# Dividing after the product instead of before it: one core's attention heads, with the reciprocals turned through DRAM

## The chip, the cores and the metric

The kernel runs on one core of one Trainium2 chip. The metric is the device time of one execution in microseconds (us). The engines are named as in the profile: PE is TensorE, DVE is VectorE, ACT is ScalarE, POOL is GpSimd, SP is the SyncE queue from which nearly all DMAs are issued.

## The reference

One decoder layer on 512 tokens of width 2048. After an RMSNorm, one projection feeds three mixers: A (8 heads of 64, three dilated windows mixed by their softmax denominators), B (a convolution of 31 taps over 512 channels, LayerNorm, swish), C (16 query heads on 2 key/value heads, window 128, one learned sink per head). The mixers' 2048 outputs go through `w_out` and are added to x; a second RMSNorm and a SwiGLU feed-forward block follow. What the change touches is the softmax of A and C, cut here to its core:

```python
p = jnp.exp(s - m[..., None])
denom = jnp.sum(p, axis=-1)
if sinks is not None:
    denom = denom + jnp.exp(sk - m)
o = jnp.einsum('nbhgqk,nbkhd->nbqhgd', p, vb)
o = o / denom_t[..., None]
```

## The kernel before, in words

All activations lie transposed: channels on the 128 partitions, the 512 tokens along the free axis. A float32 matrix product is made of three fast matmuls: each operand is split into a high and a low part (`wh`/`wl` for weights, `hh`/`hl` for the normed input, `mh_`/`ml_` for the mixers' rows), and `mm3` (L322 to L324) adds high by high, high by low and low by high.

**Stages.** The input projection makes 30 column tiles of 128 (`PROJ`); each is 16 contraction steps of three matmuls, fed by two weight units of 128 x 1024. While PE works through them, the other engines bring the mixers along in its shadow, and PE takes the small attention matmuls in between. From about 400 us on, PE does the `w_out` product: for each of 16 output tiles first the eight row tiles of `ROWS[:8]` (c0 to c6, half 0), later the other eight (a0, a1, b2, b1, b0, b3, a2, a3, half 1). The feed-forward block fills the rest, from about 580 us on.

**Order.** The order on every engine is written by a clock of the program, `Ticks`: `ticks.after(n, fn)` puts a step n ticks ahead, and the loop over matmuls calls `tick()` after every 6 of them in the projections and in half 0 of `w_out`, after every 12 in half 1. What a tick issues is appended to each engine's queue in that order, and each engine works its queue in order. A step whose input is late holds up all that stands behind it on its engine.

**A head** (`attention`, `head`) runs by one tuple of tick distances, `C_TICKS` or `A_TICKS`; their last entry `we` is the distance from the softmax weights' last split to their product with v. The steps of a head: scores on PE (`c6s`, `a0s`); maximum on DVE; exponentials on ACT into a slot `c6e` or `a0e`; the division on DVE (`packed_norm` for C, `norm` for A); transposes on PE (`c6t`, `a0t`, called flips here); split of the transposed weights into high and low (`c6hp`/`c6lp`, `a0ph`/`a0pl`), which for C are then spread by POOL's masked copies into `c6ph`/`c6pl` (L870, L873); the product with v on PE (`weigh`, L940 and L941, `c6o`, eight matmuls); copy of its two halves into `mix` by ACT (`out_high`) and DVE (L954). One row tile holds two heads, h = 0 and 1. `split_mix` (L994, L995) splits a finished row tile into `mh_`/`ml_`. For rows that come late (a2, a3), it is a tick after the row is complete.

**Slots.** Nearly every tile of 128 x 512 comes from one pool of 73 slots (`N_SLOTS`). A new tile gets a slot whose old tile has been read for the last time, and its first writer waits for that last reader. So the pool adds waits between steps that have nothing to do with each other, and which ones depends on the whole order of allocations.

**DMA.** SP issues in order. A DMA uses one of eight completion semaphores in turn and is issued when the one before it on that semaphore has landed. Small per-token factors are turned across partitions through DRAM in the kernel before already: `leave` (L642) writes a 128 x 16 tile, `back` (L647) reads it, and for keys `back` (L714) reads rows back broadcast over 64 partitions.

Of the kernel before, what the change touches and what calls it, by code (L numbers as in the profile page):

```python
# [9 lines left out]
F32 = mybir.dt.float32  # L10
# [4 lines left out]
ALU = mybir.AluOpType  # L15

P = 128
T = 512
NT = T // P
D = 2048  # L20
KT = D // P
HD = 64
HALF = (slice(0, HD), slice(HD, 2 * HD))
# [16 lines left out]
SD, KD, VD, EV = 9, 6, 12, 1  # L40


C_TICKS = (1, 6, 2, 2, 2, 3, 5, 1, 4)
A_TICKS = (0, 8, 2, 1, 3, 1, 3, 1, 5)


# [70 lines left out]
def kernel(ctx: ExitStack, tc: tile.TileContext, xT, wi, wo, wgu, wd, cst_in, outT):  # L117
    nc = tc.nc
    cp = ctx.enter_context(tc.tile_pool(name="consts", bufs=1))
# [16 lines left out]
    ticks = Ticks()  # L136

    def slot(name, dt=F32, cols=T):
        return sp.tile([P, cols], dt, name=name, tag="s")
# [11 lines left out]
    sums = defaultdict(list)  # L151
# [23 lines left out]
    def up_block(pair, m, half, j):  # L175
# [4 lines left out]
    bufs = {"A": dict(zip(("21", "11", "s", "22"), ("21a", "22a", "sa", "22b"))),  # L180
            "B": dict(zip(("21", "11", "s", "22"), ("21b", "11", "12", "sb")))}

    for n in range(2 * NBLOCKS):
# [15 lines left out]
        bufs = {c: {"21": b["22"], "11": b["21"], "s": b["s"], "22": b["11"]} for c, b in bufs.items()}  # L199
# [6 lines left out]
    for t, (g, r) in enumerate(DOWN):  # L206
# [7 lines left out]
        for k in ("21A", "11A", "21B", "11B", "22A", "22B", "12A", "12B"):  # L214
            c = k[2]
# [14 lines left out]
        bufs = {c: {"21": b["22"], "11": b["21"], "s": b["s"], "22": b["11"]} for c, b in bufs.items()}  # L230
# [255 lines left out]
    for k in range(KT):  # L486
# [9 lines left out]
        elif k < 4 or k % 2 == 0:  # L496
            wh, wl = next_unit()
            o = 0
# [294 lines left out]
    def attention(kind, box, mix, mi, heads):  # L793
        ready, every, step, s1, sx, s2, fl, ev, we = C_TICKS if kind == "c" else A_TICKS

        if mi in ROWS[-2:]:
            fl, we = fl + 2, we + 3
        name = mi
        us = UNITS[kind]
        st = {}  # L800

        def head(h):
            es = {}
            d = cp.tile([P, 4, NT], F32, name=f"{name}d{h}", tag="soft", bufs=6)
            mx, nm, den, rd = (d[:, i] for i in range(4))
            banks = {}

# [32 lines left out]
            def packed_norm():  # L840
                nc.vector.tensor_add(den, den, mx)
                nc.vector.reciprocal(rd, den)
                by = es["e"].rearrange("p (i c) -> p i c", c=P)
                nc.vector.tensor_mul(by, by, rd[:, :, None].to_broadcast([P, NT, P]))

            def packed_flip():
                b = bank(f"{name}t{h}")
# [43 lines left out]

            def norm(u):
                e = es[u]
                s = slice(us[u][0][0], us[u][-1][0] + 1)
                for i, k0, n, o in us[u]:
                    nc.vector.scalar_tensor_tensor(e[:, o:o + n], e[:, o:o + n], 1.0, mult_a[:, T - n:],
                                                   op0=ALU.mult, op1=ALU.mult, accum_out=den[:, i:i + 1])
                nc.vector.reciprocal(rd[:, s], den[:, s])
                for i, k0, n, o in us[u]:
                    nc.vector.tensor_scalar(e[:, o:o + n], e[:, o:o + n], rd[:, i:i + 1], None, op0=ALU.mult)  # L900

            ph, pl = {}, {}

# [42 lines left out]
            def out_high(b):  # L946
                if h == 0:
                    st["mix"] = slot(f"mix_{mi}")
                nc.scalar.copy(st["mix"][HALF[h]], b[HALF[1 - h]])
                ticks.after(EV, out_rows, b)  # L950

            def out_rows(b):
                m = st["mix"]
                nc.vector.tensor_add(m[HALF[h]], m[HALF[h]], b[HALF[h]])  # L954
                if h == 1:
                    mix[mi] = m
                    if late:
                        ticks.after(1, split_mix, mi)

            at_v = (len(us) - 1) * step + s1 + sx + s2 + fl + len(TBANKS[kind]) - 1 + ev + EV + we  # L960
            t0 = max(ticks.now + ready, head_at[0], box["q at"] - s1, box["k at"], box["v at"] - at_v)
            head_at[0] = t0 + every
            t0 -= ticks.now
            for u in range(len(us)):
                tu = t0 + u * step
                ticks.after(tu, scores, u)
                if kind == "c":
                    ticks.after(tu + s1, pack, u)
                    continue
                ticks.after(tu + s1, top, u)  # L970
                ticks.after(tu + s1 + sx, exps, u)
                ticks.after(tu + s1 + sx + s2, norm, u)
            tu = t0 + (len(us) - 1) * step + s1 + sx
            if kind == "c":
                ticks.after(tu, packed_exps)
                ticks.after(tu + s2, packed_norm)
                ticks.after(tu + s2 + fl, packed_flip)
            else:
                for t in range(len(TBANKS[kind])):
                    ticks.after(tu + s2 + fl + t, flip, t)  # L980
            ticks.after(t0 + at_v, weigh)

        head(0)
        head(1)


    mix, late = {}, []
# [34 lines left out]
    for name in PROJ[HEAD4:]:  # L1022
        kind, what, j = name[0], name[1], name[2:]
        if name == PROJ[-2]:
            for n, row in enumerate(ROWS[:8]):
                ticks.after(6 + n, split_mix, row)
        b = project(name)
        if kind == "b":
            ticks.after(0, glu_u if what == "u" else glu, int(j), b)
            continue  # L1030
        if kind == "c":
            box = Heads(shared) if j else shared
        else:
            box = boxes.setdefault(j, {})
        if what == "k":
            do_k(box, b, name, 1 if kind == "c" else 0)
        elif what == "v":
            do_v(box, b, name)
        else:
            do_q(box, b, name)  # L1040
        if what == "q":
            if kind == "a":
                boxes.pop(j)
            attention(kind, box, mix, kind + j, (int(j), int(j) + 8) if kind == "c" else None)
# [85 lines left out]
    for half in range(2):  # L1130
        for i, n in enumerate(OUT_ORDER[half]):
# [4 lines left out]
            for kk in range(8):  # L1136
# [4 lines left out]
                s = slice(kk * P, (kk + 1) * P)  # L1141
# [552 lines left out]
```

## Time and profile before

| | |
|---|---|
| median of 3 runs | 1843.22 us (1843.0 to 1843.69) |
| profiled execution, its own time | 1845.39 us |
| span of its trace | 1843.6 us |
| granted TensorE clock | 1.00 |
| busy: PE, DVE, ACT, POOL | 1835.2, 1445.8, 1312.1, 1026.2 us |
| DMA | 398924 packets, 334.61 MB |

The span is the time from the first to the last instruction in the trace; 1.8 us of the profiled execution lie outside it. Busy time is the sum of the durations in the records, and matmuls overlap in the array, so their records (389 ns for 128x512) are longer than the distance at which they start. Rows of the timeline give start, duration, engine, line, operation and tiles; a bracket at the end gives the idle time before the instruction and what ended it.

### The profile page before, as it was taken

The numbers are of one execution on the slowest core, as the hardware profiler recorded it, in microseconds if no ns is written. First come the engines' busy times: TensorE is split into PE (matmuls) and PEld (weight loads), VectorE is DVE, ScalarE is ACT, GpSimd is POOL, SyncE is SP. The second block draws the span as 40 slices with busy tenths as digits, with TensorE's granted clock in tenths as the row PEclk, the third lists the DMA queues.
The fourth block names the chain that finished last, engine by engine and source line by source line (L and its number), as shares of the span: only waits on it lengthen the run. The fifth ranks groups of instructions, "written<-read, shape, count | busy, mean of one in ns | idle before, by whom it ended". The sixth has DMA issues, their size and how long they took to land.

```text
span 1843.6 us, 26502 instructions
## 1 busy us (share of the span) xinstructions
PE 1835.2 (100%) x8314; PEld 1522.4 (83%) x8314; DVE 1445.8 (78%) x2063; ACT 1312.1 (71%) x1784; POOL 1026.2 (56%) x790
## 2 busy tenths in 40 slices
PE   9999999999999999999999999999999999999998
PEld 7888888888888888888888888888888888888887
DVE  6789988997689877778777787777777777777777
ACT  6345554553458788888888888888887778777775
POOL 0126644110003557886788767878676558776552
PEclk9999999999999999999999999999999999999999
DMA  7353345353343457677867778677687679877735
GB/s 276 87 150 93 87 121 153 107 161 116 124 149 103 115 151 191 188 213 182 225 187 200 201 188 226 181 209 199 182 273 258 204 225 295 257 254 260 240 119 110
DMA packets 398924, 334.61 MB, mean 181 GB/s; under 512 B 184256, under 2 KB 326720, under 8 KB 398784
## 3 DMA queue, kind: packets, MB, share of 16 engines
q1 hardware_dynamic: 398208, 332.14, 62.3%
q8 instruction: 66, 1.08, 0.3%
q10 hardware_dynamic: 576, 0.79, 0.1%
q14 instruction: 74, 0.61, 0.1%
HBM read 258.46 MB, written 65.98 MB: 176 GB/s over the span
## 4 chain that ended last, share of the span: by engine, by line
PE 95%; DVE 3%; DMA 1%; issue 0%; ACT 0%; SPq 0%; POOL 0%; DVEq 0%; POOLq 0%; ACTq 0%
PE out L1281 15%; PE out L1279 15%; PE out L1282 15%; PE out L1544 7%; PE out L1546 7%; PE out L1545 7%; PE o L322 3%; PE o L323 3%; PE o L324 3%; PE cq L322 2%; PE cq L324 2%; PE cq L323 2%; PE in L324 1%; PE in L323 1%; PE in L322 1%; PE aq L322 1%
## 5 line engine op out<-in xcount | busy, mean ns | idle before, releaser
L1279 PE MATMUL out<-wh,h 128*128 128x512 f32 x1232 | 479.2, 389 | 0.0
L1281 PE MATMUL out<-wl,h 128*128 128x512 f32 x1232 | 479.2, 389 | 0.0
L1282 PE MATMUL out<-wh,h 128*128 128x512 f32 x1232 | 479.2, 389 | 0.0
L1279 PEld LDWEIGHTS out<-wh,h 128*128 128x128 f32 x1232 | 231.2, 188 | 48.1
L1282 PEld LDWEIGHTS out<-wh,h 128*128 128x128 f32 x1232 | 231.2, 188 | 48.0
L1281 PEld LDWEIGHTS out<-wl,h 128*128 128x128 f32 x1232 | 231.2, 188 | 47.9
L1545 PE MATMUL out<-wl,a 128*128 128x512 f32 x620 | 240.4, 388 | 0.1
L1544 PE MATMUL out<-wh,a 128*128 128x512 f32 x620 | 240.4, 388 | 0.0
L1546 PE MATMUL out<-wh,a 128*128 128x512 f32 x620 | 240.3, 388 | 0.0
L289 ACT CAST wh<-w 128x1024 fp32r<-128x1024 f32 (+2 forms) x94 | 96.9, 1031 | 121.6 <-PE o L323 48.0
L1554 DVE TENSOR_TENSOR y<-y,out 128x512 f32<-128x512 f32 x192 | 128.5, 684 | 47.8 <-PE out L1546 46.1
L263 DVE TENSOR_TENSOR wl<-w,wh 128x1024 fp32r<-128x1024 f32 (+2 forms) x95 | 115.0, 1211 | 30.9 <-ACT wh L289 27.9
L1545 PEld LDWEIGHTS out<-wl,a 128*128 128x128 f32 x620 | 116.4, 188 | 24.5 <-DVE wl L285 0.5
L1546 PEld LDWEIGHTS out<-wh,a 128*128 128x128 f32 x620 | 116.4, 188 | 23.8
L1544 PEld LDWEIGHTS out<-wh,a 128*128 128x128 f32 x620 | 116.4, 188 | 23.8
L573 DVE SCALAR_TENSOR_TENSOR y<-bu,cst,y 128x511 f32<-128x511 f32 (+14 forms) x120 | 92.0, 767 | 1.3
L322 PE MATMUL o<-mh_c,wh 128*128 128x512 f32 x128 | 51.1, 399 | 0.2 <-DVE xr L1073 0.2
L322 PE MATMUL cq<-hh,wh 128*128 128x512 f32 x128 | 50.3, 393 | 0.0
L324 PE MATMUL o<-mh_c,wl 128*128 128x512 f32 x128 | 50.0, 391 | 0.0
L323 PE MATMUL o<-ml_c,wh 128*128 128x512 f32 x128 | 50.0, 390 | 0.0
L323 PE MATMUL cq<-hl,wh 128*128 128x512 f32 x128 | 49.9, 390 | 0.0
L324 PE MATMUL cq<-hh,wl 128*128 128x512 f32 x128 | 49.9, 390 | 0.0
(2351 smaller groups left out, 4766.5 us busy)
## 6 DMA issues: line engine op xcount, KB each, us to landing
od<-a SPq DMA_DIRECT2D x154, 256.0 KB
a<-od SPq DMA_DIRECT2D x154, 256.0 KB
w<-in_wi SPq DMA_DIRECT2D x58, 512.0 KB
w<-in_wo SPq DMA_DIRECT2D x32, 512.0 KB
x<-in_xT SPq DMA_DIRECT2D x16, 256.0 KB
xr<-in_xT SPq DMA_DIRECT2D x16, 256.0 KB
x2d<-xr SPq DMA_DIRECT2D x16, 256.0 KB
z<-x2d SPq DMA_DIRECT2D x64, 64.0 KB
```

What stands on the lines that cost most here:

```text
L263: fn(*args)
L289: (nc.vector.tensor_copy if u == 0 else nc.scalar.copy)(hi[:, :n], t[:, :n])
L322: nc.tensor.matmul(out, wh, xh, start=start, stop=False)
L323: nc.tensor.matmul(out, wh, xl, start=False, stop=False)
L324: nc.tensor.matmul(out, wl, xh, start=False, stop=stop)
L1279: nc.tensor.matmul(b, x[:, high], wh[:, s], start=c == f == 0 and q in (7, 1, 5, 2), stop=False, skip_group_check=True)
L1281: nc.tensor.matmul(b, x[:, high], wl[:, s], start=False, stop=False, skip_group_check=True)
L1282: nc.tensor.matmul(b, x[:, low], wh[:, s], start=False, stop=c == f == 1, skip_group_check=True)
L1544: nc.tensor.matmul(b[:, lo:hi], x[:, high], wh[:, s], start=start, stop=False, skip_group_check=True)
L1545: nc.tensor.matmul(b[:, lo:hi], x[:, high], wl[:, s], start=False, stop=False, skip_group_check=True)
L1546: nc.tensor.matmul(b[:, lo:hi], x[:, low], wh[:, s], start=False, stop=last, skip_group_check=True)
L1554: getattr(eng, op)(t, t, src)
```

## The change

The exponentials are no longer divided. `packed_norm` keeps the sum and one reciprocal per head; `norm` of A keeps the masked sums and takes one reciprocal of 128x4 for the head in place of three small ones. A tick later `sums_leave` writes the 128x4 reciprocals into a row of 512 in DRAM (element by element: neighbours in DRAM come from different partitions). When both heads of a row tile are in DRAM, `sums_back`, two ticks ahead of the second head's product with v, reads the two rows back, each broadcast over the 64 partitions of its head, into a slot `by`. A tick after the row tile is complete, `scale_out` multiplies it once by `by`, and only then is it handed on. For late rows `split_mix` follows one tick after that. `we` of C goes from 4 to 6: the products of C with v, and with them their copies, come two ticks later, and the finished row tile a third.

```diff
-C_TICKS = (1, 6, 2, 2, 2, 3, 5, 1, 4)
+C_TICKS = (1, 6, 2, 2, 2, 3, 5, 1, 6)
...
-        st = {}
+        st = {"sums": tc.dram_tile([2, T], F32, name=f"{name}sums")}
+
+        def sums_leave(h, rd):
+            nc.sync.dma_start(st["sums"][h].rearrange("(i p) -> p i", p=P), rd)
+
+        def sums_back():
+            st["by"] = slot(f"{name}by")
+            for h in range(2):
+                nc.sync.dma_start(st["by"][HALF[h]], st["sums"][h:h + 1].to_broadcast([HD, T]))
+
+        def scale_out():
+            m = st["mix"]
+            nc.vector.tensor_mul(m, m, st.pop("by"))
+            mix[mi] = m
+            if late:
+                ticks.after(1, split_mix, mi)
...
-            d = cp.tile([P, 4, NT], F32, name=f"{name}d{h}", tag="soft", bufs=6)
+            d = cp.tile([P, 4, NT], F32, name=f"{name}d{h}", tag="soft", bufs=8)
...
                 nc.vector.reciprocal(rd, den)
-                by = es["e"].rearrange("p (i c) -> p i c", c=P)
-                nc.vector.tensor_mul(by, by, rd[:, :, None].to_broadcast([P, NT, P]))
+                ticks.after(1, sums_leave, h, rd)
...
-                nc.vector.reciprocal(rd[:, s], den[:, s])
-                for i, k0, n, o in us[u]:
-                    nc.vector.tensor_scalar(e[:, o:o + n], e[:, o:o + n], rd[:, i:i + 1], None, op0=ALU.mult)
+                if u == len(us) - 1:
+                    nc.vector.reciprocal(rd, den)
+                    ticks.after(1, sums_leave, h, rd)
...
                 if h == 1:
-                    mix[mi] = m
-                    if late:
-                        ticks.after(1, split_mix, mi)
+                    ticks.after(1, scale_out)
...
             ticks.after(t0 + at_v, weigh)
+            if h == 1:
+                ticks.after(t0 + at_v - 2, sums_back)
```

In the changed file the lines of `attention` stand 13 to 15 further down: L940 and L941 become L953 and L954, DVE's addition L954 becomes L967, the scores L814 and L815 become L829 and L830, POOL's L870 and L873 become L884 and L887, the exponential L889 becomes L903, the flips L916 become L929, and `scale_out` is L812.

PE at the product of row tile c6's second head with v (`c6o`, at about 328 us before), with the scores (`a0s`) and the flips (`a0t`) of row tile a0's first two heads around it; `ak` is a projection. Before:

```order
L940 MATMUL c6o_3507<-c6ph_3414,cv_746 128x256
L941 MATMUL c6o_3507<-c6pl_3440,cv_746 128x256
L940 MATMUL c6o_3507<-c6ph_3417,cv_746 128x256
L941 MATMUL c6o_3507<-c6pl_3443,cv_746 128x256
L940 MATMUL c6o_3507<-c6ph_3417,cv_746 128x128
L941 MATMUL c6o_3507<-c6pl_3443,cv_746 128x128
L814 MATMUL a0s_3516<-ak0h_2956,aq_3097 128x384
L815 MATMUL a0s_3516<-ak0l_2957,aq_3097 128x384
L322 MATMUL ak_3392<-hh_410,wh_3304 128x512
```

The same place in the changed kernel, from the third matmul of the product on:

```order
L953 MATMUL c6o_3563<-c6ph_3438,cv_746 128x256
L954 MATMUL c6o_3563<-c6pl_3472,cv_746 128x256
L953 MATMUL c6o_3563<-c6ph_3441,cv_746 128x256
L954 MATMUL c6o_3563<-c6pl_3475,cv_746 128x256
L953 MATMUL c6o_3563<-c6ph_3441,cv_746 128x128
L954 MATMUL c6o_3563<-c6pl_3475,cv_746 128x128
L929 MATMUL a0t_3572<-ident,a0e_3392 128x128 x2
L929 MATMUL a0t_3572<-ident,a0e_3462 128x128
L929 MATMUL a0t_3572<-ident,a0e_3500 128x128
```

The product has moved past the scores and 12 projection matmuls, so that the flips of a0, which read three slots of exponentials, follow straight behind it.

POOL at the last masked copies into that product's low operand, with the semaphores that each waits for, before:

```order
L870 AFFINE_SELECT c6pl_3443<-c6lp_3412 128x2x128 [waits DMAHW4_49,DMAHW3_49,DMAHW7_49,DMAHW0_49,DVE_49]
L873 AFFINE_SELECT c6pl_3443<-c6lp_3412 128x128
L655 TENSOR_TENSOR aq1r<-aq1t 128x8 [waits DMAHW3_49]
L656 TENSOR_TENSOR aq1r<-aq1r,c_531 128x8 [waits Pool_49]
L657 TENSOR_TENSOR aq1r<-aq1r,nhalf 128x8 [waits Pool_49]
```

And in the changed kernel:

```order
L884 AFFINE_SELECT c6pl_3475<-c6lp_3436 128x2x128 [waits PE_49,Pool_49]
L887 AFFINE_SELECT c6pl_3475<-c6lp_3436 128x128
L655 TENSOR_TENSOR aq1r<-aq1t 128x8 [waits DMAHW3_49]
L656 TENSOR_TENSOR aq1r<-aq1r,c_531 128x8 [waits Pool_49]
L657 TENSOR_TENSOR aq1r<-aq1r,nhalf 128x8 [waits Pool_49]
```

The slot of `c6pl` came free by DMAs before; now it is the slot of `c6ph_3438`, and the PE count that the copy waits for is that of the third matmul of `c6o_3563`, the last to read that tile. The slot of the exponentials `a0e_3500`, which ACT writes, was freed by the third matmul of `c6o_3507` before and is freed by these POOL copies now.

DVE at the low part of a1's queries (`aq1l`), a convolution tap (`y`), and the masked sum of the exponentials `a0e_3468` of row tile a0, before:

```order
L681 TENSOR_TENSOR aq1l<-aq1raw,aq_3387 128x512 [waits Activation_49,Pool_49]
L573 SCALAR_TENSOR_TENSOR y_2941<-bu_1447,cst,y_2941 128x494
L896 SCALAR_TENSOR_TENSOR a0e_3468,a0d_3099<-a0e_3468,mult_a 128x512 [waits Activation_49]
L898 RECIPROCAL a0d_3099<-a0d_3099 128x1 [waits DVE_49]
L900 TENSOR_SCALAR a0e_3468<-a0e_3468,a0d_3099 128x512 [waits DVE_49]
```

And in the changed kernel, where the tile is `a0e_3500`:

```order
L681 TENSOR_TENSOR aq1l<-aq1raw,aq_3415 128x512 [waits DMAHW3_49,DMAHW0_49,DMAHW4_49,PE_49,DMAHW7_49,Activation_49,Pool_49]
L573 SCALAR_TENSOR_TENSOR y_2973<-bu_1448,cst,y_2973 128x494 [waits DVE_49]
L967 TENSOR_TENSOR mix_c_3486<-mix_c_3486,c6o_3453 64x512 [waits Activation_49]
L909 SCALAR_TENSOR_TENSOR a0e_3500,a0d_3133<-a0e_3500,mult_a 128x512 [waits Activation_49]
L912 RECIPROCAL a0d_3133<-a0d_3133 128x4 [waits DVE_49]
```

The division L900 is gone from here, the addition of c6's first head (L967) has come in ahead of `a0e`, and `aq1l` has a new wait for PE: its count is that of the fourth matmul of `c6o_3563`.

DVE at the end of the last row tile, a3, beside the LayerNorm of B: centring (L603), the split of row a3 (L995), the residual of an output tile (L1073) and the sum of squares (L412), before:

```order
L603 SCALAR_TENSOR_TENSOR y_2941<-lnm,y_2941 128x512
L995 TENSOR_TENSOR ml_a_4944<-mix_a_4823,mh_a_4943 128x512
L1073 TENSOR_TENSOR xr_4832<-xr_4832,o_11_4868 128x512
L412 TENSOR_TENSOR lnv<-lnv,lq_4962 128x512
L412 TENSOR_TENSOR lnv<-lnv,lq_4965 128x512
L412 TENSOR_TENSOR lnv<-lnv,lq_4968 128x512
```

And in the changed kernel:

```order
L603 SCALAR_TENSOR_TENSOR y_2973<-lnm,y_2973 128x512
L812 TENSOR_TENSOR mix_a_4839<-mix_a_4839,a3by 128x512
L1086 TENSOR_TENSOR xr_4848<-xr_4848,o_11_4887 128x512
L1008 TENSOR_TENSOR ml_a_4971<-mix_a_4839,mh_a_4970 128x512
L412 TENSOR_TENSOR lnv<-lnv,lq_4982 128x512
L412 TENSOR_TENSOR lnv<-lnv,lq_4985 128x512
```

The multiplication by the reciprocals (L812) stands behind the four centrings; ACT's high part `mh_a` of this row, which stands ahead of the squares in ACT's queue before and after, now has to wait for it.

More of the change, by code (lines that the diff above doesn't have):

```diff
@@ L893, in norm @@
                 e = es[u]
-                s = slice(us[u][0][0], us[u][-1][0] + 1)
                 for i, k0, n, o in us[u]:
```

## The prediction

> **What bounds the kernel now.** I read the page's busy times, then the chain that ended last, then the table by windows for the stage that changes, and last PE's waits within it.
>
> ```profile
> PE 1835.2 (100%) x8314; PEld 1522.4 (83%) x8314; DVE 1445.8 (78%) x2063; ACT 1312.1 (71%) x1784; POOL 1026.2 (56%) x790
> PE 95%; DVE 3%; DMA 1%; issue 0%; ACT 0%; SPq 0%; POOL 0%; DVEq 0%; POOLq 0%; ACTq 0%
> ```
>
> PE is the bound: busy for the whole span, and 95% of the chain. The change adds and removes no matmul, so the time can move only where PE waits. All edits lie in the stage of the heads, from about 100 to 500 us. There the table by windows (columns: window, its length, then busy time with count of PE, weight loads, DVE, ACT and POOL, granted clock, DMA share, GB/s) shows:
>
> ```profile
> 100.00:200.00 100.00, 99.19 (x507) 83.95 (x506) 90.87 (x180) 54.39 (x125) 48.53 (x66) 1.00 0.38 110
> 200.00:300.00 100.00, 100.00 (x513) 84.94 (x512) 87.45 (x164) 52.68 (x119) 52.89 (x83) 1.00 0.45 117
> 300.00:400.00 100.00, 99.54 (x493) 83.53 (x492) 92.38 (x223) 53.39 (x95) 20.76 (x32) 1.00 0.50 133
> 400.00:500.00 100.00, 99.80 (x477) 82.89 (x476) 73.00 (x157) 42.27 (x62) 4.76 (x4) 1.00 0.39 127
> ```
>
> PE idles for 0.8, 0, 0.5 and 0.2 us in these four hundreds. DVE, at 87 to 92% in three of them, is the next engine, but it is a shadow: what it does late costs nothing until PE asks for it. PE's waits from 100 to 480 us name every place (total us, times, longest):
>
> ```profile
> PE c1o L941 <- POOL c1pl L873: 0.8, 2, 0.5
> PE a0t L916 <- DVE a0e L900: 0.3, 1, 0.3
> PE o L322 <- DVE xr L1073: 0.2, 1, 0.2
> PE a1t L916 <- DVE a1e L900: 0.2, 1, 0.2
> ```
>
> That is the most the change can give: 1.5 us of waits, and the restart of PE behind each. Against 1843 us it is below 0.2% (3.7 us), about what a measurement of this kernel can tell from no change. So a gain that can be measured is all but excluded, and the question is what new waits appear.
>
> **What goes: the division.** Three rows give its price on DVE, with one of the additions to `mix` as the nearest shape for the new multiplication.
>
> ```profile
> L844 DVE TENSOR_TENSOR c0e<-c0e,c0d x2: 691/692/692, 124.3 to 132.5; 128x512 f32<-128x512 f32 x2
> L900 DVE TENSOR_SCALAR a0e<-a0e,a0d x8: 288/384/485, 320.6 to 345.5; 128x128 f32<-128x128 f32 x2, 128x256 f32<-128x256 f32 x2, 128x384 f32<-128x384 f32 x2, 128x512 f32<-128x512 f32 x2
> L954 DVE TENSOR_TENSOR mix_a<-mix_a,a0o x2: 672/682/692, 357.0 to 371.7; 64x512 f32<-64x512 f32 x2
> ```
>
> DVE loses 16 x 0.69 = 11.1 us (C, both heads of 8 row tiles) and 32 x 0.38 = 12.2 us (A), and gains 12 x 0.69 = 8.3 us of `scale_out`: 15 us less of some 340. On PE's path this is worth only the two flip waits, a0t and a1t, which stand behind L900: the last flip waits for multiply, reciprocal and division, and the last two are now off that path.
>
> **What moves: C's product with v.** Two ticks are 12 matmuls. The wait of 0.8 us at c1o, where POOL's copies end late, gets that long to disappear:
>
> ```profile
> 183.55 0.28 PE L940 MATMUL c1o<-c1ph,cv 128*128 128x256 f32 x1
> 184.34 0.39 PE L941 MATMUL c1o<-c1pl,cv 128*128 128x256 f32 x1 [0.52 <-POOL c1pl L873]
> 185.37 0.39 PE L941 MATMUL c1o<-c1pl,cv 128*128 128x256 f32 x1 [0.29 <-POOL c1pl L873]
> 185.77 0.45 PE L322 MATMUL cq<-hh,wh 128*128 128x512 f32 x1
> 327.87 0.28 PE L940 MATMUL c6o<-c6ph,cv 128*128 128x256 f32 x1
> 328.10 0.28 PE L940 MATMUL c6o<-c6ph,cv 128*128 128x256 f32 x1
> 328.46 0.28 PE L941 MATMUL c6o<-c6pl,cv 128*128 128x256 f32 x1
> 328.75 0.39 PE L814 MATMUL a0s<-ak0h,aq 128*128 128x384 f32 x1
> ```
>
> The eight matmuls of c1o take 185.77 - 183.55 = 2.22 us, those of c6o, unhindered, 328.75 - 327.87 = 0.88. So c1o gives 1.3 us, which includes about 0.11 us for each restart. a1t gives 0.2 + 0.1. Together **-1.6 us**.
>
> **What comes: c6's second head.** The pool of slots is full here, and the order of allocation now makes POOL's last copies into `c6pl`, ACT's exponentials `a0e` and DVE's `aq1l` wait for this product (the change's rows on POOL and DVE). What these steps take:
>
> ```profile
> 327.65 0.41 POOL L870 TENSOR_SCALAR_AFFINE_SELECT c6pl<-c6lp 128x256 fp32r<-128x256 f32 x1
> 328.00 0.29 POOL L873 TENSOR_SCALAR_AFFINE_SELECT c6pl<-c6lp 128x128 fp32r<-128x128 f32 x1
> 328.33 0.69 DVE L681 TENSOR_TENSOR aq1l<-aq1raw,aq 128x512 fp32r<-128x512 f32 x1 [0.91 <-POOL c6pl L873]
> 328.42 0.78 ACT L889 ACTIVATE a0e<-a0s,a0d,aq0r 128x512 f32<-128x512 f32 x1 [3.90 <-PE c6o L940]
> 328.94 0.73 DVE L573 SCALAR_TENSOR_TENSOR y<-bu,cst,y 128x494 f32<-128x494 f32 x1
> 329.58 0.68 DVE L896 SCALAR_TENSOR_TENSOR a0e<-a0e,mult_a 128x512 f32<-128x512 f32 x1
> 331.88 0.60 PE L916 MATMUL a0t<-ident,a0e 128*128 128x128 f32 x4
> ```
>
> Before, the exponentials had from 328.42 to 331.88 until the flips; now the flips follow the product at once. I count from the start of its third matmul. It is read to the end at 0.28; POOL's two copies end 0.64 later (328.00 + 0.29 - 327.65), with 0.1 of handing over at about 1.05. The sixth matmul, due at 0.36 (328.46 - 328.10), waits for them: 0.7, and 0.1 of restart. The exponential ends at about 1.9. On DVE `aq1l` starts at 0.4, takes until 1.0, the tap until 1.65 (0.64 from start to start), the addition of c6's first head until 2.3, and the masked sum of `a0e` until 2.95. The fourth flip, due at 0.65 + 0.8 + 3 x 0.09 = 1.7, waits 1.25, and 0.1 of restart. Together **+2.15 us**. If DVE stood ready and only POOL's copies counted it would be 0.8; if each handing over took 0.3 us rather than 0.1, 3.0. The flips of a0's second head, at 346 us, lose their old wait of 0.3 but find DVE later by the same additions and by c6's `scale_out` of 0.69: **+0.3 us**, between -0.4 and +0.7.
>
> **What comes: row a3 beside the LayerNorm.**
>
> ```profile
> 471.02 0.61 ACT L994 CAST mh_a<-mix_a 128x512 fp32r<-128x512 f32 x1
> 472.06 2.48 DVE L603 SCALAR_TENSOR_TENSOR y<-lnm,y 128x512 f32<-128x512 f32 x4 [2.00 <-PE lnm L601]
> 473.38 1.83 ACT L411 ACTIVATE lq<-y 128x512 f32<-128x512 f32 x3
> 475.66 2.28 DVE L412 TENSOR_TENSOR lnv<-lnv,lq 128x512 f32<-128x512 f32 x3
> 478.68 0.60 PE L472 MATMUL lv<-ident,lnv 128*128 128x128 f32 x4
> L322 PE MATMUL o<-mh_a,wh x64: 389/389/389, 493.2 to 579.6; 128*128 128x512 f32 x64
> ```
>
> ACT's `mh_a` stood at 471.02, ahead of squares (the first, L408, and the three of L411) that had to wait for DVE's centrings anyway. Now it waits for `scale_out`, which starts at 474.5 behind the centrings: 475.2 to 475.8, then the four squares (0.61 each, 1.83 / 3) until 478.2, DVE's last sum until 478.95. In the trace the sums end at 477.94 and the transposes L472 start 0.74 later. So PE waits 478.95 + 0.1 - 478.68, about 0.4, with the restart 0.5; the next transposes of this chain, with about as little to spare, may lose 0.15. Together **+0.65 us**, between 0 and 1.5. Row a3 itself is not late: the first product with A's rows starts at 493.2.
>
> **What comes: the DMAs.** 24 writes of 512 elements of 4 B, and 24 broadcast reads of 64 x 2 KB, all on SP. The nearest rows are a write of 16 B pieces and its return, and a broadcast of rows:
>
> ```profile
> 125.63 1.74 SPq L642 DMA_DIRECT2D cq1d<-cq1p  x4
> 129.39 0.34 SPq L647 DMA_DIRECT2D cq1t<-cq1d  x1
> 132.62 0.60 POOL L655 TENSOR_TENSOR cq1r<-cq1t 128x8 f32<-128x8 f32 x1 [12.74 <-DMA cq1t<-cq1d]
> 95.26 1.12 SPq L714 DMA_DIRECT2D ckwide<-cke  x2
> 99.34 0.75 DVE L723 SCALAR_TENSOR_TENSOR ckk<-ckraw,gqk,ckwide 128x512 f32<-128x512 f32 x1
> q1 hardware_dynamic: 398208, 332.14, 62.3%
> ```
>
> The write's four parts, 512 packets like the new write's, had landed when the return was issued, 3.8 us after the first; the broadcast, used 4.1 us after its first issue, bounds the other from above. The write has at least nine ticks before `sums_back` (a tick of six matmuls is 1.4 us). `sums_back` stands five ticks ahead of `scale_out` at the least (two to the product, one to the copy, one to the addition, one to the multiplication): 6.8 us, against 4.1. So the multiplication finds its factors, with 2.7 us to spare where it is tightest. The 13,824 new packets at 0.623 x 16 x 1843.6 / 398208 = 0.046 us are 40 us on each of 16 engines, of some 350 us in which these are 38 to 50% busy: room enough. SP issues about 1 us more per pair, some 24 us in all; queued behind are weight loads, for which there are eight buffers at one unit per 5.5 us. I take **0**, between 0 and +2.
>
> The Trainium skill, page "DMA: Bandwidth & Descriptors", speaks against this part: its section "Rules for kernel authors" has a last dimension that is not contiguous become one descriptor per element, and its "Specifications" say that transfers below 512 B make the DMA read, modify and write. The row of 16 B pieces, below that size too, landed within 3.8 us. If the rule doubled this, an estimate, the write would take 7.6 us and still be back in its nine ticks.
>
> **The sum.** -1.6 + 2.15 + 0.3 + 0.65 + 0 = +1.5 us. The trace belongs to an execution of 1845.39 us (span 1843.6, and 1.8 outside it), which becomes 1846.9; the median without the profiler stood 2.2 below it, so I forecast 1843.2 + 1.5 = **1844.7 us**.
>
> **Rivals.**
>
> *Only the gains.* The slot waits fall elsewhere or DVE, relieved of 15 us, runs early enough to have them done. For it: DVE's lower load. Against it: the waits are on PE's own matmuls, which relief on DVE doesn't bring forward. Then -1.6 and -0.4 at a0t: 1841.2 us. Chance 0.2, within the same 0.2%.
>
> *The factors return late (slower).* The 4 B writes hold the queues up, and `sums_back` lands after `scale_out` is due. DVE then stands at L812 with the low parts of weights, taps and flips behind it. It decides from 6.8 us of return on. At 10 us, two and a half times the row above, DVE loses 3.2 us at each of the three tightest row tiles (c2, c7, a1) and less at others, some 10 us, of which the 8 to 12 idle us per hundred take about half: +5, 1849.7 us with the other terms. For it: the pieces are four times smaller than any here. Against it: the equal packet count. Chance 0.08. By the rule of the Trainium skill named above ("DMA: Bandwidth & Descriptors", section "Specifications"), were it to slow the pieces by over 2.5, this is the case that results.
>
> *The full pool bites elsewhere as well (slower).* Each wait on another's last reader costs about the 2 us worked out at c6; two more such places give +5.5 in all, 1848.7. Against it: PE has no wait from 200 to 300 us, and elsewhere the steps moved have ticks to spare. Chance 0.07.
>
> My forecast has 0.65. Eight in ten lie from 1841.0 (only the gains) to 1848.4 (upper bounds of c6 at +0.85, a3 at +0.85, flips at +0.4, and +1.6 of DMA). Slower by over 0.2% (above 1846.9) takes both slower rivals nearly whole: 0.14. Faster by over 0.2% (below 1839.5) would need more than all waits of the stage: 0.02. The same: 0.84.
>
> **What would show it.** Right: PE's list of waits without c1o and a1t, with c6o behind POOL's `c6pl` (about 0.7), a0t behind DVE's `a0e` (about 1.2), and `lv` behind `lnv` (about 0.4); DVE busy some 15 us less from 100 to 500 us; L812 without a wait for a DMA. Wrong: L812 waiting on `by`, a wait of PE for weights, PE waits over 4 us in all between 100 and 500 us, or any change in the feed-forward block.

## The result and the profile after

| | before | changed |
|---|---|---|
| median, us | 1843.45 (1842.93 to 1845.19, 6 runs) | 1902.84 (1892.96 to 1911.31, 6 runs) |
| ratio, 95% interval | | 1.032 (1.0293 to 1.0348) |
| span of the trace, us | 1843.6 | 1890.9 |
| granted TensorE clock, mean | 1.00 | 0.991 |

The change costs 59 us; the forecast was 1.5. The profiled execution of the changed kernel is the quickest of the six (1892.96 us), so its trace shows the smallest loss, 47.3 us of span. The page's busy row and the row of the DMA queue:

```profile
PE 1850.2 (98%) x8314; PEld 1530.2 (81%) x8314; DVE 1429.9 (76%) x2011; ACT 1312.5 (69%) x1784; POOL 1021.9 (54%) x790
q1 hardware_dynamic: 412800, 335.33, 66.9%
```

DVE lost 16 us, where 15 were forecast. PE does the same 8314 matmuls but is no longer busy throughout. The queue's packets took 0.669 x 16 x 1890.9 us, 1,860 us more than before, for 14,592 more packets of 3 MB together. The windows of the heads' stage, in the same columns as before:

```profile
100.00:200.00 100.00, 97.44 (x487) 81.90 (x486) 79.96 (x161) 51.95 (x121) 37.68 (x61) 0.98 0.63 98
200.00:300.00 100.00, 88.90 (x427) 73.67 (x426) 67.14 (x132) 39.46 (x92) 41.58 (x64) 0.95 0.75 94
300.00:400.00 100.00, 85.89 (x396) 69.85 (x395) 73.74 (x158) 42.27 (x79) 31.35 (x51) 0.93 0.62 120
400.00:500.00 100.00, 94.45 (x459) 78.43 (x457) 74.17 (x176) 48.79 (x81) 9.11 (x8) 0.98 0.69 136
```

PE does less in each hundred us. From 100 to 300 us so do DVE, ACT and POOL, and some of their work slides into the hundreds behind. The DMA engines are busy 62 to 75% of the time in place of 38 to 50%, and yet move fewer bytes a second: 112 GB/s in the mean of the four hundreds in place of 122. From 200 to 300 us, where PE had no wait at all, it idles for 11 us. The granted clock (the third column from the end) falls below 1 as well. PE's longest waits from 100 to 540 us:

```profile
PE c4s L829 <- DMA cq<-cq4l: 6.6, 1, 6.6
PE c6o L954 <- POOL c6pl L887: 5.6, 4, 3.9
PE c4o L953 <- POOL c4ph L887: 3.0, 1, 3.0
PE a1t L929 <- DVE a1e L909: 3.0, 1, 3.0
PE o L322 <- DVE xr L1086: 2.5, 1, 2.5
PE c4o L954 <- POOL c4pl L887: 2.5, 3, 1.4
PE c6s L829 <- DMA cq<-cq6l: 2.2, 1, 2.2
PE c5o L953 <- POOL c5ph L887: 2.0, 1, 2.0
```

Two of them are for plain transfers of queries (`cq<-cq4l`, `cq<-cq6l`), which the change does not touch. All 16 rows of this list sum to 33.6 us; 17.9 of them are for POOL's copies. POOL works its queue in order, and ahead of the copies it stands where per-token factors come back from DRAM (three rows of its list of waits, others left out):

```profile
POOL ak2wide L655 <- DMA ak2t<-ak2d: 16.1, 1, 16.1
POOL cq6r L655 <- DMA cq6t<-cq6d: 7.9, 1, 7.9
POOL cq4r L655 <- DMA cq4t<-cq4d: 7.8, 1, 7.8
```

In the trace before, POOL waits 1.9 us for `cq4t` and not at all for the other two. How much of the 17.9 us comes from these returns was not worked out further. SP's queue shows where such a transfer gets stuck; here the first write of reciprocals (L803) and what SP issues behind it (two rows of the queries' transfers, between the second and the third, are left out):

```profile
122.19 0.37 SPq L803 DMA_DIRECT2D c0sums<-c0d  x1
122.83 1.74 SPq L642 DMA_DIRECT2D cq1d<-cq1p  x4
125.82 0.59 SPq L243 DMA_DIRECT2D w<-in_wi  x1
135.75 0.34 SPq L647 DMA_DIRECT2D cq1t<-cq1d  x1
136.14 1.40 SPq L243 DMA_DIRECT2D w<-in_wi  x1
```

Before, the return L647 was issued 3.8 us after the write L642 began. Now it is 12.9 us, since SP waits for `cq1d` to land. By the landing events the four DMAs of this L642, right behind the first write, land 9.4 to 11.7 us after their issue, where they took 1.4 to 1.5 before. SP's list of waits has this too, with the broadcast reads waiting for the writes they read:

```profile
SPq L647 <- DMA cq1d<-cq1p: 9.2, 2, 8.8
SPq L808 <- DMA c5sums<-c5d: 6.9, 2, 6.0
```

By the trace's landing events the 24 writes of reciprocals land 11.2 us after their issue (median; 8.3 to 19.0), where I had put 3.8. The 4 B packets themselves take 9 ns in the records (median; the longest 1.2 us). It is others that grow: the 11,520 packets of 4 KB, which carry weights, go from 199 to 319 ns in the mean and from 1.5 to 10.2 us for the longest.

The rest of the loss is the clock. In its worst 20 us PE has 12.57 us of work at a granted clock of 0.83:

```profile
300.00:320.00 20.00, 12.57 (x51) 9.57 (x50) 13.54 (x23) 8.59 (x14) 8.99 (x16) 0.83 0.66 137
```

Six times in this stage the records of the clock show it at one half, for 3.4 or 6.8 us, each time behind waits of PE: 30.7 us in all, in which 15.4 us of work are lost. 33.6 + 15.4 = 49.0 us, less the 1.5 us of the old waits, is 47.5, and the trace is 47.3 us longer.

### The profile page after: what moved, and what is told of

It is laid out like the page before. It is cut to its first block, busy times and chain, and to the rows that moved or that the text cites. A ratio compares the mean times of both kernels' runs of the same rounds, so it can differ in the third digit from the quotient of the medians.

```text
span 1890.9 us, 26517 instructions
## 1 busy us (share of the span) xinstructions
PE 1850.2 (98%) x8314; PEld 1530.2 (81%) x8314; DVE 1429.9 (76%) x2011; ACT 1312.5 (69%) x1784; POOL 1021.9 (54%) x790
## 4 chain that ended last, share of the span: by engine, by line
PE 71%; DVE 1%; DMA 0%; issue 0%; ACT 0%; DVEq 0%; SPq 0%
PE out L1292 15%; PE out L1295 15%; PE out L1294 15%; PE out L1558 7%; PE out L1557 7%; PE out L1559 7%; PE o L322 2%; PE o L323 2%; PE o L324 2%; DVE y L1567 0%; DVE wl L285 0%; DMA out_T<-z 0%; DVE z L1466 0%; DVE lnv L412 0%; DVE y L1536 0%
## 5 line engine op out<-in xcount | busy, mean ns | idle before, releaser
L1567 DVE TENSOR_TENSOR y<-y,out 128x512 f32<-128x512 f32 x192 | 128.6, 684 | 47.5 <-PE out L1559 45.6
```

The source lines that it names most:

```text
L1567: getattr(eng, op)(t, t, src)
```

## Experiments

Three theories. W: the writes of 4 B pieces hold up the DMA queues, and everything else follows. O: the moved products and the waits for slots lose the time. B: the broadcast reads do.

**Pieces of 16 B.** The same bytes and the same reads, laid down in another order, so that the factors read back belong to other tokens.

```diff
-nc.sync.dma_start(st["sums"][h].rearrange("(i p) -> p i", p=P), rd)
+nc.sync.dma_start(st["sums"][h].rearrange("(p i) -> p i", i=NT), rd)
```

> The changed kernel with the reciprocals laid down in DRAM in the order in which the partitions hold them: 128 pieces of 16 B in place of 512 of 4 B, the same bytes, the same instructions on every engine, the same reads back. It multiplies by reciprocals of other tokens, so its values are not the reference's. Theory W (the writes of 4 B pieces hold up the DMA queues, and all that lands late, PE waiting and its clock falling follows from that): the loss goes, 1844 us within 4, clock 1.00, and PE's waits from 100 to 540 us fall from 32 us to under 5. Theory O (the moved products and the waits for slots lose the time): 1890 to 1910 as before. Theory B (the broadcast reads lose it): 1890 to 1910 too.

Measured: 1847.59 us against 1843.58, ratio 1.0018 (1.0009 to 1.0027). One rearranged write takes away all but 4 us of the 59. The 24 writes land in 2.9 us (median; 1.4 to 5.3) in place of 11.2. PE's waits:

```profile
PE c6o L954 <- POOL c6pl L887: 1.1, 1, 1.1
PE a0t L929 <- DVE a0e L909: 0.8, 1, 0.8
PE lv L472 <- DVE lnv L412: 0.5, 1, 0.5
```

These three are the places that the prediction named. Theories O and B fall for the 55 us, since order and reads are those of the changed kernel.

**The writes alone.** The kernel before, with only the 24 writes added, which nobody reads (the diff is cut to the write; the small tiles that hold the reciprocals also get 8 buffers for 6, as in the change).

```diff
+nc.sync.dma_start(st["sums"][h].rearrange("(i p) -> p i", p=P), rd)
```

> The kernel before with nothing but the 24 writes added: division, order and the products' place stay, and each head's reciprocals go to DRAM in 512 pieces of 4 B, where nobody reads them. Theory W: most of the loss is there, 1870 to 1900 us, and DMAs behind a write land 5 to 10 us later. Theories O and B: 1843 to 1845 us.

Measured: 1886.18 us, ratio 1.0229 (1.021 to 1.0248). So the writes alone cost 43 us, with the division still in place and no product moved. The 17 us from there to the changed kernel were not split; they go too when the pieces are 16 B long, as the first experiment shows. PE's waits here have the same transfers and copies in them:

```profile
PE c6s L817 <- DMA cq<-cq6l: 7.6, 1, 7.6
PE o L322 <- DVE xr L1079: 6.4, 1, 6.4
PE c6o L947 <- POOL c6pl L877: 5.0, 3, 2.8
```

A write also delays what is issued after it through its completion semaphore, of which there are eight in turn. Here SP holds a load of weights (L243) until the write has landed, though nobody reads it:

```profile
SPq L243 <- DMA c7sums<-c7d: 6.3, 1, 6.3
```

**The products back in their place.**

```diff
-C_TICKS = (1, 6, 2, 2, 2, 3, 5, 1, 6)
+C_TICKS = (1, 6, 2, 2, 2, 3, 5, 1, 4)
```

> The changed kernel with the last entry of C_TICKS back at 4, so that C's products with v stand where they stood before. Theory O: the loss shrinks to under 10 us, below 1853. Theory W: it stays, 1890 to 1920 us, as the products only lose two ticks of room. Theory B: it stays too, or grows by a few us since the reads have the same distance to the multiplication.

Measured: 1895.08 us, ratio 1.0277 (1.0259 to 1.0296). Moving C's products is not what costs the most. That it is 8 us under the changed kernel's median is within the 18 us by which that one's runs differ, so up to 8 us for the move are neither shown nor excluded.

**Reciprocals turned by DVE first.** The change with rows of 128 B on their way to DRAM (the diff is cut to the turn and the write).

```diff
-            nc.sync.dma_start(st["sums"][h].rearrange("(i p) -> p i", p=P), rd)
+            nc.vector.transpose(w[:, 32:64], w[:, :32])
+            ticks.after(1, sums_leave, w)
...
+            for a in range(4):
+                nc.sync.dma_start(st["sums"][:, 32 * a:32 * a + 32], w[32 * a:32 * a + 2 * NT, 32:64])
```

> The change with another way to DRAM: the reciprocals of both heads of a row tile are turned by one DVE transpose of 32x32 blocks, and leave a tick later in four DMAs of eight rows of 128 B; reads back, multiplication and order as in the changed kernel. Theory W: 1841 to 1847 us, since the prediction's sum without the writes was 1843.2 + 1.5. Theory O and B: 1890 to 1910.

Measured: 1846.86 us, ratio 1.0016 (1.0007 to 1.0025). This is the change with its DMA term near nothing (12 short transposes on DVE and 24 more writes, which land in 1.2 us, come in), so it tests the other terms. PE's list of waits reads as in the first experiment, and the timeline shows the two at c6's second head:

```profile
330.22 0.28 PE L968 MATMUL c6o<-c6ph,cv 128*128 128x256 f32 x1
331.55 0.39 PE L969 MATMUL c6o<-c6pl,cv 128*128 128x256 f32 x1 [1.05 <-POOL c6pl L901]
331.95 0.52 PE L944 MATMUL a0t<-ident,a0e 128*128 128x128 f32 x3
333.28 0.43 PE L944 MATMUL a0t<-ident,a0e 128*128 128x128 f32 x1 [0.82 <-DVE a0e L923]
```

The product's sixth matmul and the fourth flip wait, as worked out. What I had left out follows them:

```profile
320.00:340.00 20.00, 18.13 (x87) 14.92 (x86) 14.04 (x35) 12.11 (x22) 3.00 (x7) 0.91 0.54 143
```

The clock stands at one half for 3.4 us, from 333.4 on, which costs 1.7 us. The trace of the first experiment has the same fall, at 334.4.

**What makes the writes slow.** Five versions of the writes alone, added to the kernel before. Theories W1 to W4, named in the expectations, say what a write is slow for. The diffs are against the writes alone. First, each piece of 4 B to its own 64 B of DRAM:

```diff
-st = {"sums": tc.dram_tile([2, T], F32, name=f"{name}sums")}
+st = {"sums": tc.dram_tile([2, T, 16], F32, name=f"{name}sums")}
...
-nc.sync.dma_start(st["sums"][h].rearrange("(i p) -> p i", p=P), rd)
+nc.sync.dma_start(st["sums"][h].rearrange("(i p) c -> p i c", p=P)[:, :, 0], rd)
```

> The kernel before with the 24 writes added as in the run of the writes alone (1886 us), but each of the 512 pieces of 4 B goes to its own 64 B of DRAM, where the run before packed them side by side in 2 KB. Theory W1 (a piece of 4 B costs its 20 ns wherever it lies): 1875 to 1895 us. Theory W2 (what costs is that neighbouring pieces, which come from different partitions, fall into the same stretch of memory): 1843 to 1850 us, with weight packets no longer than before.

Then 512 pieces of 16 B side by side (`T, 4` for `T, 16`, and the whole tile `d` written):

> The kernel before with 24 writes added of 512 pieces of 16 B, packed side by side, neighbours from different partitions (all four small columns of a head instead of the reciprocals alone). Theory W1: a piece of 16 B in the kernel before lands fast, so 1843 to 1850 us. Theory W2: four neighbours still share 64 B and 512 pieces are written, so a quarter of the loss or more: 1853 to 1886 us.

Then a quarter of the pieces of 4 B, side by side (`[:, :1]` on both sides of the write):

> The kernel before with 24 writes added of 128 pieces of 4 B side by side (one reciprocal per partition in place of four). Both theories: the clog of one write falls with the count of its pieces, from 10 us to 2 or 3, which the queues' room covers: 1843 to 1850 us. If a write costs its time whatever its count: 1880 to 1890 us.

And, when these had come out, 4 B pieces 8 B and 16 B apart (`T, 2` and `T, 4`):

> The kernel before with 24 writes of 512 pieces of 4 B, each piece 8 B after its neighbour, so that 8 fall into 64 B (16 side by side cost 43 us, 1 per 64 B cost 1.6, 4 pieces of 16 B per 64 B cost 2). Theory W3 (pieces that fall into the same 64 B are written one after the other, about 0.5 us each, so the depth counts and not the number): half the delay of a write, landing about 4 us later than alone, and 1846 to 1868 us. Theory W4 (only pieces that touch each other side by side collide): 1843 to 1847 us.

> The same with each piece 16 B after its neighbour, 4 to a stretch of 64 B. Theory W3: about 2 us later than alone, within the queues' room: 1843 to 1848 us. Theory W4: 1843 to 1847 us. If pieces of 4 B collide over a wider stretch than 64 B, unlike those of 16 B: above 1855 us.

Landing is the median of the 24 writes from issue to landing event, with the least and the greatest; the time is the difference of the medians. The two slowest versions have two runs each, the others eight.

| write | pieces to 64 B | landing, us | time over before, us | ratio, interval |
|---|---|---|---|---|
| 512 of 4 B side by side | 16 | 10.6 (9.0 to 18.9) | 42.6 | 1.0229 (1.021 to 1.0248) |
| 128 of 4 B side by side | 16 | 8.8 (7.2 to 12.2) | 25.2 | 1.0134 (1.0115 to 1.0152) |
| 512 of 4 B, 8 B apart | 8 | 4.9 (3.0 to 7.2) | 2.9 | 1.0016 (1.0005 to 1.0027) |
| 512 of 4 B, 16 B apart | 4 | 3.5 (2.5 to 5.1) | 1.4 | 1.0005 (0.9994 to 1.0016) |
| 512 of 16 B side by side | 4 | 3.4 (2.3 to 4.9) | 2.1 | 1.0007 (0.9997 to 1.0017) |
| 512 of 4 B, 64 B apart | 1 | 2.7 (1.8 to 3.7) | 1.6 | 1.0004 (0.9993 to 1.0014) |

Theory W1, a price for each piece of 4 B wherever it lies, had 1875 to 1895 us for the pieces 64 B apart, and 1845.25 was measured. Theory W2, a price for neighbours in the same stretch, had 1853 to 1886 us for the pieces of 16 B, and 1845.69 was measured. The quarter surprised both (1843 to 1850 us): I expected a cost that falls with the count, and a fourth of the pieces lands in 8.8 us against 10.6 and leaves 25 of the 43 us. Neither count nor size alone decides. What orders the landings is how many pieces of one write share 64 B; where that is the same, the count still moves the time. SP's queue with the writes side by side, and then with the same number of the same pieces spaced, where the return L647 is issued 8 us earlier (rows between the second and the third left out):

```profile
124.31 0.37 SPq L803 DMA_DIRECT2D c0sums<-c0d  x1
125.66 1.74 SPq L642 DMA_DIRECT2D cq1d<-cq1p  x4
137.53 0.34 SPq L647 DMA_DIRECT2D cq1t<-cq1d  x1
```

```profile
124.47 0.37 SPq L803 DMA_DIRECT2D c0sums<-c0d  x1
125.82 1.75 SPq L642 DMA_DIRECT2D cq1d<-cq1p  x4
129.59 0.34 SPq L647 DMA_DIRECT2D cq1t<-cq1d  x1
```

The last two times lie within the ranges of both theories left, so only the landings tell them apart. Theory W3 (pieces within the same 64 B go one after the other) has the order right; its 0.5 us a piece is too much from 1 to 8 (0.3) and too little from 8 to 16 (0.7). Theory W4 (only pieces that touch collide) does not explain why 8 B apart lands 2.2 us later than 64 B apart. The unit of 64 B was not varied, so it stays open whether it is that, or another length. Nor was it varied that the neighbours come from different partitions. The mechanism behind the order is therefore not shown.

**A version against the writes and the three waits.** Turned reciprocals (the diff is against that version), with what the traces point to against the three waits: 74 slots, C's products one tick later than before and not two, the LayerNorm two ticks later.

```diff
-T_LN = 250
+T_LN = 252
...
-C_TICKS = (1, 6, 2, 2, 2, 3, 5, 1, 6)
+C_TICKS = (1, 6, 2, 2, 2, 3, 5, 1, 5)
...
-N_SLOTS = 73
+N_SLOTS = 74
...
-    wides = [cp.tile([P, 64], F32, name=f"wide{i}") for i in range(4)]
+    wides = [cp.tile([P, 64], F32, name=f"wide{i}") for i in range(3)]
```

> The version with turned reciprocals (1846.9 us) with 74 slots in place of 73 (three tiles for turning in place of four make the room), the last entry of C_TICKS at 5, and the LayerNorm of B two ticks later. The waits left in that version, 1.1 us at c6's product, 0.8 at a0's flips, 0.5 at the LayerNorm's transposes, and the 3.4 us of half clock behind the first two, should all go: PE without a wait over 0.3 us from 100 to 540 us and 1841.5 to 1843.0 us, 0.5 to 2 us under the kernel before. If the pool's waits only move to other places: 1844 to 1847 us.

Measured: 1842.52 us against 1843.64, ratio 0.9993 (0.9984 to 1.0002). One wait of PE is left from 100 to 540 us, longer than the 0.3 expected at most:

```profile
PE o L322 <- DVE xr L1101: 0.6, 1, 0.6
```

So the division after the product works, and with its waits removed the kernel comes out about 1 us faster, somewhat less than the 1.5 us of waits that stood there before; the interval does not tell this from nothing. Nor is it the division's alone: the kernel before was not run with 74 slots and the later LayerNorm.

## Why the prediction was wrong, point by point

- **What bounds the kernel, and the most that can be won: right.** PE was the bound and its waits of 1.5 us the ceiling; the best version came out 1.1 us faster, which its interval does not tell from nothing.
- **The DMAs: the step that failed.** I took 0, at most +2. The sum went by packets ("512 packets like the new write's") and by busy time at 0.046 us a packet. The rows that I compared with, L642 and L714, have pieces of 16 B, 64 B apart within one DMA, and rows of 2 KB. Neither puts 16 pieces of one DMA into the same 64 B, so they bounded nothing from above. Measured: 11.2 us to land in place of 3.8, and the four DMAs right behind the first write held up as long (9.4 to 11.7 us).
- **The late rival: the right cause, with most of the price left out.** It named the 4 B writes but let only `scale_out` wait for them, some 10 us of DVE, of which half was to reach PE. That part came nearly in size, at other row tiles than c2, c7 and a1: `scale_out` waits 8.5 us in all, with DVE idle:

```profile
  DMA c0by<-c0sums: 4.6, 1
  DMA a0by<-a0sums: 3.2, 1
  DMA c4by<-c4sums: 0.5, 1
  DMA c1by<-c1sums: 0.2, 1
```

  Most of the price is paid by what stands behind a write in the queues: queries (8.8 us of PE's waits) and per-token scales, at which POOL stands. The experiment without any `scale_out` shows it, at +43 us. PE has no wait of its own for weights, though their packets grow. I gave a chance of 0.08 to 1849.7, and the range ended at 1848.4. Of the signs of being wrong that the prediction named, two came: L812 waits on `by`, and PE's waits are over 4 us.
- **The page against the change.** The Trainium skill, "DMA: Bandwidth & Descriptors", section "Specifications", has transfers below 512 B read, modify and write. I doubled the landing by it and found it hidden. The direction was right; but by size alone, pieces of 4 B 64 B apart should be as slow as those side by side, and they land in 2.7 us against 10.6. The measurement decides.
- **c6's second head: right in place and nearly in size.** PE idles 1.05 us at the product and 0.82 at the flip in the trace of the turned version. Counted from the start that was due, as the prediction did, the delays are 1.2 and 1.1 us, worked out as 0.7 and 1.25. The LayerNorm's transposes wait 0.5 against 0.4. The +0.3 at the second flips and the +0.15 behind the LayerNorm did not come. c1o and a1t are gone from that trace, as forecast.
- **A term that was missing: the clock.** Waits of PE were priced at their length. Two waits of together 1.9 us within 3.4 us brought half clock for 3.4 us, another +1.7. With it the sum of +1.5 becomes +3.2, and the turned version measures +3.3. That these agree to 0.1 is luck: two terms of +0.45 together did not come, c6 cost some 0.3 more than worked out, and single runs of the turned version lie from 1844.5 to 1848.4 us.

## What to carry to other kernels

Before a small transfer is costed by its nearest row, compare the pattern in memory too, not only count and size: how many separately written pieces share a stretch of 64 B. Its price is then to be looked for in the transfers queued behind it, not in its own consumer. And where PE is the bound, two short waits close together may cost more than their sum: here 1.87 us of waits within 3.4 us were followed by half clock, worth another 1.7 us.

## What the runs showed of the hardware that was not expected

- Writing 512 B in 128 pieces of 4 B side by side, from 128 partitions, takes 8.8 us to land and holds up other DMAs; 8 KB in 512 pieces of 16 B take 3.4 us.
- A write that clogs shows next to nothing in its own packets (9 ns in the median). It shows in the packets of other DMAs in flight, up to 10.2 us for 4 KB of weights, and in the landing of small writes behind it (9.4 to 11.7 us in place of 1.4 to 1.5).
- The clock fell to one half behind waits of 1.05 and 0.82 us that lie 0.9 us apart, and did not behind those of 0.52 and 0.29 us at c1o in the kernel before. The Trainium skill, "TensorE: Matmul & The Clock Gate", section "Part 1: The HAM clock gate (the "warmup" mystery)", has half rate come after an idle window of about 3.4 us. The length of the slow stretches agrees (3.4 us or a multiple of it), but in the turned version PE had idled for only 1.87 of the 3.41 us before it set in. The twelve traces of this case bear out a share, not a gap: cut into stretches of 3.41 us, on the grid that the clock's records keep, full clock is followed by half clock after all 19 stretches with 1.85 us of idle PE or more, after 5 of the 12 with 1.44 to 1.77, and after none with 1.41 or less.
